# Operand offsets, kept output weights, a sixth early gate/up tile and the place of the second norm's sums in a fp32 decoder layer

## The chip, the cores and the metric

The kernel runs on one NeuronCore of a Trainium2 chip. The metric is the device time of one execution in microseconds, from the first instruction to the last and what the launch adds around them. The kernel before was timed in three runs.

## What is computed

One decoder layer over 512 positions with 2048 channels, in fp32. It takes a norm, projects to q, k, v and u, mixes with attention (8 heads) and with a state space model that a gate follows, projects both halves back with `w_out`, and adds to the residual `h`. Then follow the second norm, a gated MLP of 5632 channels, and the final norm:

```python
hn = _rmsnorm(h, norm1_g)
q, k, v, u = jnp.split(hn @ w_in, [1024, 2048, 3072], axis=-1)
attn_out = _dilated_attention_mixer(q, k, v, cos, sin)
ssm_out = _s5_mixer(u, ...)          # y * sigmoid(y @ w_glu + b_glu)
h = h + jnp.concatenate([attn_out, ssm_out], axis=-1) @ w_out
hn = _rmsnorm(h, norm2_g)
h = h + (jax.nn.silu(hn @ w_gate) * (hn @ w_up)) @ w_down
return _rmsnorm(h, final_g)
```

## The kernel before

**Layout and precision.** Activations lie transposed: 128 channels on the partitions, 512 positions in the free dimension. Every fp32 operand of a projection is held as two fp32r parts, hi and lo; `split` (lines 89 to 91) makes them, hi by a copy on ScalarE, lo by a subtraction on VectorE through the helper `tt` (line 50). `mm3` (lines 108 to 111) is then three matmuls: weights' hi against the activations' hi, hi against lo, lo against hi. So every weight costs a DMA, a copy on ScalarE and a subtraction on VectorE before TensorE has it.

**Slots.** Activations' hi and lo lie in slots of 1088 floats, given out by `laid` (pool, tag, count, offset) and `slot`; the last argument is the offset in floats at which the operand starts inside its slot. Offsets 0 and 48 are multiples of 16 floats (64 bytes); 4, 8, 40 and 52 are not. The text calls the first kind aligned and the second odd.

**Stages on TensorE**, in the order of time of the profiled execution: u, q, k and v to about 451 us, attention to 492 (pieces of it), `glu` 492 to 537 (operand `ysp`, offset 4), `oa` 537 to 627 (the attention half of `w_out`, operand `attn`, offset 8), `os0` and `os1` 627 to 723 (its other half, operand `ssm`, offset 40, for the first and the second 256 positions), then the MLP. `os0` and `os1` each load and split all 16 tiles of this half of `w_out`: `wchunk` (lines 103 to 106) loads 512 KB and splits it in two pieces of 512 columns.

**The second norm.** After each `os` tile the residual tile `h` gets the product on VectorE, ScalarE squares it, and GpSimd (`pool`) adds the square to the sums `ss2`. When a half is complete, `rstd_of` sums over the partitions with tiny matmuls (`ss_20`, `ss_21`, line 146), works out the reciprocal root on VectorE and ScalarE (`rst`), puts it on a diagonal (`dg`), and one matmul by a matrix of ones spreads it over the partitions (`bc`, line 159); ScalarE copies that to `rstd2`.

**The MLP.** Gate and up of a tile are made together by a scheme with seven products A to G of half the size, over operands `c1` (A, B), `c4` (C), `c2`, `c3` (D to G). Each product takes 24 matmuls of 256 columns, in two halves `hh` of 12. `c1` needs only the first half of the positions, so it is made in `first_half` during `os1`; `c2`, `c3` and `c4` need the second half. While these wait for the second norm, TensorE runs products A and B of the first NEARLY = 5 tiles (`gu_first`); weights of the first two are split ahead during `os1` (`split_early`). In the loop over `k` (the lines that follow `first = ...`), VectorE makes the normed pieces `x2` and `t34` (line 59), GpSimd makes four differences per k from them, and `split` makes `c2`, `c3`, `c4`. Then come the tiles' other products, and after every fourth tile the products with `w_down` (`dn`), 11 phases in all.

**What sets the order.** Engines run in order. The order on each is set by the tile scheduler from the program, by data dependences and the count of buffers in each tag; nothing in the kernel before fixes the place of the norm's matmuls among the products of `gu_first`.

## Time and profile before

| | |
|---|---|
| median of three runs | 2098.67 us (2095.85 to 2101.73) |
| the profiled execution's own time | 2100.22 us |
| its span, first to last instruction | 2098.4 us |
| mean granted TensorE clock | 0.986 |
| TensorE busy, matmuls | 2053.3 us (98%), 13522 instructions |
| VectorE busy | 1533.5 us (73%) |
| ScalarE busy | 865.5 us (41%) |
| GpSimd busy | 74.6 us (4%), 82 instructions |

The shares are means over the whole program. TensorE is busy nearly throughout; the rows to look for are those stretches where it is not, and those where its matmuls follow one another more slowly than elsewhere. In the traces a matmul's own duration covers its way through the array, so its rate is read from the distance of one start to the next. The same holds on VectorE, where one operation's end overlaps the next one's start.

### The profile page before, as it was taken

Reading aid. Unit: us, or ns where it says so; the run is one execution under the profiler, and the core shown is the slowest. Engines: PE = TensorE matmul, PEld = TensorE weight load, DVE = VectorE, ACT = ScalarE, POOL = GpSimd, SP = SyncE. Lnnn points to the kernel's source line nnn. Section 1 sums busy time; section 2 is a strip of 40 time slices with the busy share of each in tenths; the row PEclk is TensorE's granted clock in tenths of the full one; section 3 lists DMA queues with packets and bytes.
Section 4 is the critical chain, followed back from the end, with each engine's and each line's share of the span. In section 5 each row is a group of like instructions: output and inputs, shape, how many; then the busy total and the mean of one; then the engine's idle time right before and its main releaser. Section 6 shows DMA issues by size and latency. Waiting matters only on the chain.

```text
span 2098.4 us, 35067 instructions
## 1 busy us (share of the span) xinstructions
PE 2053.3 (98%) x13522; PEld 1859.9 (89%) x13522; DVE 1533.5 (73%) x2974; ACT 865.5 (41%) x1523; POOL 74.6 (4%) x82
## 2 busy tenths in 40 slices
PE   8999999999999979999999999999999999999996
PEld 6888888877889979899999989899998989999896
DVE  8845897565436899686786868687785868778686
ACT  6222222265225545353443525344353535444354
POOL 0000000000002360000000000000000000000002
PEclk9989999999999989999999999999999999999998
DMA  7533234424325523333232333323232332323232
GB/s 235 167 107 113 91 105 145 124 95 154 111 97 188 183 71 132 111 108 124 91 122 81 119 101 103 121 85 128 91 121 81 119 103 102 121 89 124 91 122 81
DMA packets 117192, 244.23 MB, mean 116 GB/s; under 512 B 39040, under 2 KB 57312, under 8 KB 117024
## 3 DMA queue, kind: packets, MB, share of 16 engines
q1 hardware_dynamic: 107808, 239.88, 34.0%
q10 hardware_dynamic: 9216, 2.10, 0.5%
q8 instruction: 106, 1.74, 0.3%
q14 instruction: 62, 0.51, 0.1%
HBM read 229.77 MB, written 9.03 MB: 114 GB/s over the span
## 4 chain that ended last, share of the span: by engine, by line
PE 91%; DVE 5%; issue 2%; ACT 1%; DMA 1%; POOL 0%; SPq 0%; DVEq 0%; ACTq 0%; POOLq 0%
PE gu L109 13%; PE gu L111 13%; PE gu L110 12%; PE dn L110 7%; PE dn L109 7%; PE dn L111 7%; PE q L111 1%; PE q L110 1%; PE u L109 1%; PE u L110 1%; PE lps L435 1%; PE q L109 1%; PE u L111 1%; PE oa L109 1%; PE oa L111 1%
## 5 line engine op out<-in xcount | busy, mean ns | idle before, releaser
L110 PE MATMUL dn<-m,whi_dn 128*128 128x512 f32 x640 | 249.0, 389 | 0.0
L111 PE MATMUL dn<-m,wlo_dn 128*128 128x512 f32 x640 | 248.8, 389 | 0.0
L109 PE MATMUL dn<-m,whi_dn 128*128 128x512 f32 x640 | 248.8, 389 | 0.0
L50 DVE TENSOR_TENSOR h<-h,dn 128x512 f32<-128x512 f32 x160 | 110.0, 687 | 172.5 <-PE dn L111 171.5
L90 ACT ACTIVATE whi_dn<-raw_dn 128x512 fp32r<-128x512 f32 x160 | 100.9, 632 | 240.1 <-PE dn L110 208.2
L50 DVE TENSOR_TENSOR raw_r<-raw_r,raw_r 128x512 f32<-128x512 f32 x264 | 182.8, 692 | 2.1
L111 PEld LDWEIGHTS dn<-m,wlo_dn 128*128 128x128 f32 x640 | 120.1, 188 | 25.0
L109 PEld LDWEIGHTS dn<-m,whi_dn 128*128 128x128 f32 x640 | 120.1, 188 | 24.6
L110 PEld LDWEIGHTS dn<-m,whi_dn 128*128 128x128 f32 x640 | 120.1, 188 | 24.5
L50 DVE TENSOR_TENSOR wlo_dn<-raw_dn,whi_dn 128x512 fp32r<-128x512 f32 x160 | 109.8, 687 | 17.2 <-ACT whi_dn L90 16.2
L109 PE MATMUL gu<-c,whi_D 128*128 128x256 f32 x352 | 98.4, 280 | 3.2 <-ACT whi_D L90 3.2
L109 PE MATMUL gu<-c,whi_C 128*128 128x256 f32 x352 | 99.8, 284 | 1.6 <-ACT c L90 1.6
L109 PE MATMUL gu<-c,whi_E 128*128 128x256 f32 x352 | 98.9, 281 | 2.5 <-ACT whi_F L90 1.1
L111 PE MATMUL gu<-c,wlo_E 128*128 128x256 f32 x352 | 98.8, 281 | 2.5 <-DVE wlo_E L50 2.4
L111 PE MATMUL gu<-c,wlo_D 128*128 128x256 f32 x352 | 98.7, 280 | 1.7 <-DVE wlo_D L50 1.7
L111 PE MATMUL gu<-c,wlo_C 128*128 128x256 f32 x352 | 99.5, 283 | 0.5 <-DVE wlo_C L50 0.5
L110 PE MATMUL gu<-c,whi_C 128*128 128x256 f32 x352 | 99.5, 283 | 0.1
L110 PE MATMUL gu<-c,whi_E 128*128 128x256 f32 x352 | 98.3, 279 | 0.0
L110 PE MATMUL gu<-c,whi_D 128*128 128x256 f32 x352 | 98.2, 279 | 0.0
L109 PE MATMUL gu<-c,whi_F 128*128 128x256 f32 x352 | 97.9, 278 | 0.0
L110 PE MATMUL gu<-c,whi_F 128*128 128x256 f32 x352 | 97.9, 278 | 0.0
L111 PE MATMUL gu<-c,wlo_F 128*128 128x256 f32 x352 | 97.7, 278 | 0.0
(317 smaller groups left out, 6462.1 us busy)
## 6 DMA issues: line engine op xcount, KB each, us to landing
raw_r<-w_gu SPq DMA_DIRECT2D x176, 512.0 KB, 3.5
raw_dn<-w_down SPq DMA_DIRECT2D x80, 512.0 KB, 4.0
raw_os<-w_out SPq DMA_DIRECT2D x32, 512.0 KB, 3.4
raw_q<-w_q SPq DMA_DIRECT2D x16, 512.0 KB, 4.1
raw_k<-w_k SPq DMA_DIRECT2D x16, 512.0 KB, 3.4
raw_v<-w_v SPq DMA_DIRECT2D x16, 512.0 KB, 3.8
raw_oa<-w_out SPq DMA_DIRECT2D x16, 512.0 KB, 3.5
raw_u<-w_u SPq DMA_DIRECT2D x15, 512.0 KB, 5.8
```

The source lines that it names most:

```text
L50: (eng or dve).tensor_tensor(out=out, in0=in0, in1=in1, op=op)
L90: act.activation(hi, raw, AF.Copy)
L109: pe.matmul(ps, wh, x[:, 0, :], start=first, stop=False)
L110: pe.matmul(ps, wh, x[:, 1, :], start=False, stop=False)
L111: pe.matmul(ps, wl, x[:, 0, :], start=False, stop=last)
L435: pe.matmul(lps[:, g, :], tm_[:, :, :, g].rearrange("p i q -> p (i q)"), U[:, 8 * b + g, :], start=True, stop=True)
```

## The change

1. **Offsets.** `ysp` goes from 4 to 0, `attn` from 8 to 0, `ssm` from 40 to 52 for the first two of eight and 48 for the others. `c4` went to offset 52 in all four slots; now only `c4_0` does, the single odd slot.
2. **Kept output weights.** Tiles 10 to 15 of the `ssm` half of `w_out` are split once, in `os0`, in pieces of 1024 columns, and kept; `os1` runs these six first and then tiles 0 to 9. Six loads of 512 KB and twelve pairs of 512-column splits go from `os1`.
3. **Sixth early tile.** NEARLY is 6. Tile 5 has no bank to keep, so ScalarE copies its A and B sums to `ev5`. Its 48 matmuls move ahead of the first tile's C. Three tiles' weights, not two, are split ahead during `os1`.
4. **The sums' place.** `rstd_of` marks the last sums matmul and the spread matmul. Products of half (0, 1) of the early tiles are issued after the sums, all later ones after the spread; those of (0, 0) are free.
5. **GpSimd's work.** The 30 additions to `ss2` and the 32 differences in the loop over `k` go to VectorE.

```diff
--- before.py
+++ after.py
@@ -1,6 +1,7 @@
 
 
 
+import contextlib
 import math
 
 import numpy as np
@@ -138,12 +139,14 @@
             act.activation(sq, src, AF.Square)
             tt(acc_t, acc_t, sq, ALU.add)
 
+    marks = {}
+
     def rstd_of(acc_t, out, name):
 
         n = acc_t.shape[-1] // 128
         ps = aux([128, 4], "ss_" + name)
         for m in range(n):
-            pe.matmul(ps[:, m:m + 1], acc_t[:, 128 * m:128 * m + 128], ones[:, 0:1], start=True, stop=True)
+            sums = pe.matmul(ps[:, m:m + 1], acc_t[:, 128 * m:128 * m + 128], ones[:, 0:1], start=True, stop=True)
         st = cpool.tile([128, 4, 4], F32, tag="rst", name="rst_" + name)
         v, q, r, c = (st[:, i, :n] for i in range(4))
         ts(v, ps[:, :n], 1.0 / D, EPS, ALU.mult, ALU.add)
@@ -156,7 +159,8 @@
         for m in range(n):
             ts(dg[:, m, :], ident, c[:, m:m + 1])
         bc = aux([128, 512], "bc_" + name)
-        pe.matmul(bc[:, :128 * n], ones, dg[:, :n].rearrange("p m t -> p (m t)"), start=True, stop=True)
+        spread = pe.matmul(bc[:, :128 * n], ones, dg[:, :n].rearrange("p m t -> p (m t)"), start=True, stop=True)
+        marks[name] = sums.ins, spread.ins
         act.activation(out, bc[:, :128 * n], AF.Copy)
         return c
 
@@ -560,7 +564,7 @@
     for b in range(8):
         yt = wpool.tile([128, 512], F32, tag="sq", name=f"yt{b}", bufs=4)
         nc.sync.dma_start(yt, sy[b].rearrange("p i c -> p (i c)"))
-        t_ = laid(ring2, "B", f"ysp{b}", 8, 4)
+        t_ = laid(ring2, "B", f"ysp{b}", 8, 0)
         split(t_[:, 0, :], t_[:, 1, :], yt)
         ysp.append(t_)
 
@@ -600,7 +604,7 @@
                 act.activation(PT[:, :w], tp[:, :w], AF.Copy)
             else:
                 pe.matmul(po[:, 128 * j:512], vs[j][:, 128 * h:128 * h + 128], PT[:, :w], start=j == 0, stop=j == 3)
-        o = slot("A0", f"attn{h}", 8)
+        o = slot("A0", f"attn{h}")
         act.activation(o[:, 0, :], po, AF.Copy)
         tt(o[:, 1, :], po, o[:, 0, :].bitcast(F32), ALU.subtract)
         attn.append(o)
@@ -616,7 +620,7 @@
         nc.sync.dma_start(yt, sy[f].rearrange("p i c -> p (i c)"))
         z = wpool.tile([128, NC_, T], F32, tag="sq", name=f"gz{f}", bufs=4)
         tt(z.rearrange("p c i -> p i c"), yt.rearrange("p (i c) -> p i c", i=T), g_.rearrange("p (i c) -> p i c", i=T), ALU.mult)
-        o = slot("A1", f"ssm{f}", 40)
+        o = slot("A1", f"ssm{f}", 52 if f < 2 else 48)
         split(o[:, 0, :], o[:, 1, :], z.rearrange("p c i -> p (c i)"))
         ssm.append(o)
     closed("v")
@@ -638,9 +642,20 @@
     rstd2 = ss2
     mp = opened("mlp", bufs=1)
 
+    KEEP = (10, 11, 12, 13, 14, 15)
+    kept = {}
+
+    def keep(f):
+        at = ("B", ring2, 8) if KEEP.index(f) < 4 else ("C", mp, 4)
+        hl = [laid(at[1], at[0], f"{t}_kept{f}", at[2], 0).rearrange("p a b -> p (a b)") for t in ("hi", "lo")]
+        raw = wraw(a["w_out"][2 * f + 1], f"os_{f}")
+        split(hl[0], hl[1], raw)
+        kept[f] = [[t[:, 512 * i:512 * i + 512] for t in hl] for i in range(2)]
+        return kept[f]
+
     def comb(tag, name, pool_=None, bufs=8):
 
-        return laid(pool_ or ring, tag, name, bufs, 52 if tag == "C" else 48).rearrange("p a (h t) -> p a h t", h=2)
+        return laid(pool_ or ring, tag, name, bufs, 52 if name == "c4_0" else 48).rearrange("p a (h t) -> p a h t", h=2)
 
     early = {}
 
@@ -654,7 +669,7 @@
         raw = load_first(f, hh)
         early[f, hh] = []
         for i in range(2):
-            t_ = laid(ring2, "B", f"w{'AB'[i]}{f}_{hh}", 8, 0)
+            t_ = laid(*((ring2, "B") if f < 2 else (mp, "C")), f"w{'AB'[i]}{f}_{hh}", 8 if f < 2 else 4, 0)
             split(t_[:, 0], t_[:, 1], raw[:, 512 * i:512 * i + 512])
             early[f, hh].append((t_[:, 0], t_[:, 1]))
 
@@ -674,28 +689,28 @@
         split(t_[:, :, 0, :], t_[:, :, 1, :], n1[k][0])
         c1.append(t_)
 
-    PRE = (2, 3, 4, 5)
-    AT = (4, 5, 6, 7, 8, 9, 10, 11)
+    PRE = (1, 2, 3, 4, 11, 12)
+    AT = (3, 4, 5, 6, 7, 8, 9, 10)
     for e in range(2):
         es = E[e]
-        for f in range(KT):
+        for i, f in enumerate(KEEP + tuple(range(KEEP[0])) if e else range(KT)):
             ps = acc(f"os{e}_{f}")
-            ws = wchunk(a["w_out"][2 * f + 1], f"os{e}_{f}")
+            ws = (kept[f] if e else keep(f)) if f in KEEP else wchunk(a["w_out"][2 * f + 1], f"os{e}_{f}")
             for k in range(8):
                 hi, lo = ws[k // 4]
                 sl = slice(128 * (k % 4), 128 * (k % 4) + 128)
                 mm3(ps[:, 0:256], hi[:, sl], lo[:, sl], ssm[k][:, :, es], k == 0, k == 7)
             tt(h[f][:, es], h[f][:, es], ps[:, 0:256], ALU.add)
-            if f == 0:
+            if i == 0:
                 act.activation(ss2[:, es], h[f][:, es], AF.Square)
             else:
                 sq = wpool.tile([128, 512], F32, tag="sq", name=f"sq_h{e}_{f}", bufs=4)[:, 0:256]
                 act.activation(sq, h[f][:, es], AF.Square)
-                tt(ss2[:, es], ss2[:, es], sq, ALU.add, pool)
-            if e == 1 and f in PRE:
-                split_early(PRE.index(f) // 2, PRE.index(f) % 2)
-            if e == 1 and f in AT:
-                first_half(AT.index(f))
+                tt(ss2[:, es], ss2[:, es], sq, ALU.add)
+            if e == 1 and i in PRE:
+                split_early(PRE.index(i) // 2, PRE.index(i) % 2)
+            if e == 1 and i in AT:
+                first_half(AT.index(i))
         rstd_of(ss2[:, es], rstd2[:, es], f"2{e}")
 
     PR = {1: (c1, 0), 2: (c1, 1), 3: (c2, 0), 7: (c2, 1), 5: (c3, 0), 6: (c3, 1), 4: (c4, None)}
@@ -720,15 +735,21 @@
     def gu_first(f):
 
         bk = bank(f"gu{f}_0")
+        sums, spread = marks["21"]
         for hh in range(2):
             if (f, hh) in early:
                 wa, wb = early[f, hh]
             else:
                 raw = load_first(f, hh)
                 wa, wb = wsplit(raw[:, W0], f"A{f}_{hh}"), wsplit(raw[:, W1], f"B{f}_{hh}")
-            product([bk], 1, hh, *wa)
-            product([bk], 2, hh, *wb)
-        return bk
+            with tc.issue_after(sums if (f, hh) == (0, 1) else spread) if (f, hh) != (0, 0) else contextlib.nullcontext():
+                product([bk], 1, hh, *wa)
+                product([bk], 2, hh, *wb)
+        if f < NBANK:
+            return bk
+        out = wpool.tile([128, 512], F32, tag="ev", name=f"ev{f}")
+        act.activation(out, bk, AF.Copy)
+        return out
 
     def gu(f, bank0=None):
         banks = [bank0 or bank(f"gu{f}_0")] + [bank(f"gu{f}_{i}") for i in range(1, 4)]
@@ -766,7 +787,8 @@
         split(o[:, 0, :], o[:, 1, :], g_)
         return o
 
-    NEARLY = 5
+    NEARLY = 6
+    NBANK = 5
     NPH = 11
     first = [gu_first(f) for f in range(NEARLY)]
     for k in range(8):
@@ -774,14 +796,14 @@
         x_, y_, z_ = (wpool.tile([128, 2, 256], F32, tag="sq", name=f"{n}_{k}", bufs=4) for n in ("x2", "t12", "t34"))
         norm(x_[:, 0], k + 8, es)
         norm(z_[:, 0], k, es)
-        tt(x_[:, 1], x_[:, 0], z_[:, 0], ALU.subtract, pool)
+        tt(x_[:, 1], x_[:, 0], z_[:, 0], ALU.subtract)
         t2 = comb("B", f"c2_{k}", ring2)
         split(t2[:, :, 0, :], t2[:, :, 1, :], x_)
-        tt(y_[:, 0], z_[:, 0], n1[k][0][:, 0], ALU.subtract, pool)
-        tt(y_[:, 1], x_[:, 0], y_[:, 0], ALU.subtract, pool)
+        tt(y_[:, 0], z_[:, 0], n1[k][0][:, 0], ALU.subtract)
+        tt(y_[:, 1], x_[:, 0], y_[:, 0], ALU.subtract)
         t3 = comb("A1", f"c3_{k}")
         split(t3[:, :, 0, :], t3[:, :, 1, :], y_)
-        tt(z_[:, 1], n1[k][0][:, 1], y_[:, 1], ALU.subtract, pool)
+        tt(z_[:, 1], n1[k][0][:, 1], y_[:, 1], ALU.subtract)
         if k % 2 == 0:
             t4 = comb("C", f"c4_{k}", mp, 4)
             c4.append(t4)
```

How this moves instructions, at three places. On TensorE before, at the sums of the second half (`gu0` is the first early tile, `c1` its operand):

```order
L109 MATMUL gu0_0_6935<-c1_7_6760,wA0_1_6383 128x256
L110 MATMUL gu0_0_6935<-c1_7_6760,wA0_1_6383 128x256
L111 MATMUL gu0_0_6935<-c1_7_6760,wA0_1_6383 128x256
L146 MATMUL ss_21_6919<-ones_71,ss2_5575 128x1 x2
L109 MATMUL gu0_0_6935<-c1_4_6627,wB0_1_6386 128x256
L110 MATMUL gu0_0_6935<-c1_4_6627,wB0_1_6386 128x256
```

The sums stand behind the 36 matmuls of products A and B of the first tile's first half and A of its second; the spread matmul `bc_21` stands 37 matmuls further on. On TensorE after:

```order
L111 MATMUL os1_9_6814<-ssm7_4981,whi_os1_9_1_6821 128x256
L112 MATMUL os1_9_6814<-ssm7_4981,wlo_os1_9_1_6822 128x256
L112 MATMUL gu0_0_6869<-c1_2_6415,wB0_0_6255 128x256
L110 MATMUL gu0_0_6869<-c1_3_6459,wB0_0_6255 128x256
L111 MATMUL gu0_0_6869<-c1_3_6459,wB0_0_6255 128x256
L112 MATMUL gu0_0_6869<-c1_3_6459,wB0_0_6255 128x256
L149 MATMUL ss_21_6853<-ones_71,ss2_5575 128x1 x2
L110 MATMUL gu0_0_6869<-c1_4_6504,wA0_1_6290 128x256
L111 MATMUL gu0_0_6869<-c1_4_6504,wA0_1_6290 128x256
```

Of the 24 matmuls of tile 0's first half, 20 now stand inside `os1`, and four between its last matmul and the sums; the spread matmul stands 24 matmuls further on, and the other five early tiles' 240 matmuls behind it. On VectorE before, from the diagonal of the second norm on (`x2` and `t34` are the normed pieces, `wlo_` the low parts of weights):

```order
L54 TENSOR_SCALAR dg_21_6929<-ident_70,rst_21_6922 128x128 x2
L50 TENSOR_TENSOR wlo_B3_0_7113<-raw_g3_0_7105,whi_B3_0_7112 128x512
L50 TENSOR_TENSOR wlo_A3_1_7144<-raw_g3_1_7140,whi_A3_1_7143 128x512
L59 SCALAR_TENSOR_TENSOR x2_0_7246<-h_4990,g2_67,ss2_5575 128x256
L59 SCALAR_TENSOR_TENSOR t34_0_7248<-h_4990,g2_67,ss2_5575 128x256
L59 SCALAR_TENSOR_TENSOR x2_1_7264<-h_4990,g2_67,ss2_5575 128x256
L50 TENSOR_TENSOR c2_0_7252<-x2_0_7246,c2_0_7252 128x2x256
L59 SCALAR_TENSOR_TENSOR t34_1_7266<-h_4990,g2_67,ss2_5575 128x256
L50 TENSOR_TENSOR c3_0_7257<-t12_0_7247,c3_0_7257 128x2x256
```

The four differences per k are not in this list, as they run on GpSimd. On VectorE after, up to the first step of the reciprocal root:

```order
L51 TENSOR_TENSOR ss2_5575<-ss2_5575,sq_h1_7_6772 128x256
L51 TENSOR_TENSOR h_4990<-h_4990,os1_9_6814 128x256
L51 TENSOR_TENSOR wlo_A4_0_7092<-raw_g4_0_7088,whi_A4_0_7091 128x512
L51 TENSOR_TENSOR ss2_5575<-ss2_5575,sq_h1_8_6811 128x256
L51 TENSOR_TENSOR ss2_5575<-ss2_5575,sq_h1_9_6850 128x256
L57 TENSOR_SCALAR rst_21_6856<-ss_21_6853 128x2
```

The last two additions of squares now stand behind a split of `gu4` weights on VectorE. And from the diagonal on:

```order
L55 TENSOR_SCALAR dg_21_6863<-ident_70,rst_21_6856 128x128 x2
L60 SCALAR_TENSOR_TENSOR x2_0_7231<-h_4990,g2_67,ss2_5575 128x256
L60 SCALAR_TENSOR_TENSOR t34_0_7233<-h_4990,g2_67,ss2_5575 128x256
L51 TENSOR_TENSOR x2_0_7231<-x2_0_7231,t34_0_7233 128x256
L51 TENSOR_TENSOR t12_0_7232<-t34_0_7233,n1_0_6334 128x256
L60 SCALAR_TENSOR_TENSOR x2_1_7249<-h_4990,g2_67,ss2_5575 128x256
L51 TENSOR_TENSOR t12_0_7232<-x2_0_7231,t12_0_7232 128x256
L51 TENSOR_TENSOR c2_0_7237<-x2_0_7231,c2_0_7237 128x2x256
L51 TENSOR_TENSOR t34_0_7233<-n1_0_6334,t12_0_7232 128x256
```

No weights' split stands between the diagonal and `x2_0` any more, and the subtractions that GpSimd had stand between the normed pieces and the splits.

## Rows read from the trace of the kernel before

**Rows 1.** The page, part 1: busy time, share of the span and instructions.

```profile
PE 2053.3 (98%) x13522; PEld 1859.9 (89%) x13522; DVE 1533.5 (73%) x2974; ACT 865.5 (41%) x1523; POOL 74.6 (4%) x82
```

**Rows 2.** Stretches: us, busy time (instructions) PE PEld DVE ACT POOL, granted clock, DMA share, GB/s.

```profile
676.00:733.20 57.20, 55.24 (x456) 54.10 (x455) 48.89 (x94) 34.10 (x68) 16.84 (x16) 1.00 0.54 186
733.20:784.00 50.80, 39.81 (x262) 37.00 (x261) 47.03 (x65) 22.84 (x42) 33.62 (x32) 0.81 0.20 66
784.00:844.00 60.00, 57.81 (x478) 56.37 (x478) 57.59 (x107) 30.59 (x51) 0.00 (x0) 0.99 0.38 137
```

**Rows 3.** Timeline about the second norm, all engines: start, us, engine, line, operation.

```profile
722.92 0.28 PE L109 MATMUL gu<-c,wA 128*128 128x256 f32 x1
...
724.93 0.41 DVE L50 TENSOR_TENSOR h<-h,os 128x256 f32<-128x256 f32 x1
...
726.00 0.73 POOL L50 TENSOR_TENSOR ss<-ss,sq_h 128x256 f32<-128x256 f32 x1 [1.53 <-ACT sq_h L693]
...
727.16 0.50 PE L146 MATMUL ss<-ones,ss 128*128 128x1 f32 x4
...
728.99 0.48 DVE L54 TENSOR_SCALAR dg<-ident,rst 128x128 f32<-128x128 f32 x2
...
731.97 0.60 PE L159 MATMUL bc<-dg,ones 128*128 128x256 f32 x2
...
733.25 0.48 DVE L59 SCALAR_TENSOR_TENSOR x<-h,g,ss 128x256 f32<-128x256 f32 x1
```

**Rows 4.** VectorE's groups by form from 733.2 to 784: busy, mean ns | idle before.

```profile
L50 DVE TENSOR_TENSOR c<-x,c 128x512 fp32r<-128x512 f32 x8 | 7.7, 957 | 3.0 <-ACT c L90 3.0
...
L50 DVE TENSOR_TENSOR c<-t,c 128x256 fp32r<-128x256 f32 x8 | 5.5, 683 | 0.0
```

**Rows 5.** Timeline of VectorE from 766 to 771.

```profile
769.37 0.68 DVE L50 TENSOR_TENSOR wlo_C<-raw_r,whi_C 128x512 fp32r<-128x512 f32 x1
769.97 0.41 DVE L50 TENSOR_TENSOR c<-t,c 128x256 fp32r<-128x256 f32 x1
770.31 0.68 DVE L50 TENSOR_TENSOR raw_r<-raw_r,raw_r 128x512 f32<-128x512 f32 x1
```

**Rows 6.** Timeline of VectorE at the end of the stretch.

```profile
844.18 0.69 DVE L50 TENSOR_TENSOR wlo_G<-raw_r,whi_G 128x512 fp32r<-128x512 f32 x1 [0.18 <-ACT whi_G L90]
```

**Rows 7.** Tiles k, oa, glu and os on TensorE: ns min/median/max, first and last start.

```profile
L110 PE MATMUL k<-x,whi_k x113: 389/389/389, 261.7 to 337.9; 128*128 128x512 f32 x113
...
L109 PE MATMUL oa<-attn,whi_oa x128: 391/395/397, 537.6 to 626.5; 128*128 128x512 f32 x128
...
L110 PE MATMUL glu<-ysp,whi_glu x50: 390/394/398, 499.7 to 533.7; 128*128 128x512 f32 x50
...
L109 PE MATMUL os<-ssm,whi_os x130: 282/283/283, 629.4 to 675.8; 128*128 128x256 f32 x130
```

**Rows 8.** Timeline of TensorE in a later tile: first matmul of A, C, B and D.

```profile
909.65 0.28 PE L109 MATMUL gu<-c,whi_A 128*128 128x256 f32 x1
...
911.01 0.28 PE L109 MATMUL gu<-c,whi_C 128*128 128x256 f32 x1
...
912.43 0.28 PE L109 MATMUL gu<-c,whi_B 128*128 128x256 f32 x1
...
913.81 0.28 PE L109 MATMUL gu<-c,whi_D 128*128 128x256 f32 x1
```

**Rows 9.** Timeline of TensorE after a wait, from 806 to 810.

```profile
806.37 0.36 PE L109 MATMUL gu<-c,whi_E 128*128 128x256 f32 x1 [0.75 <-ACT whi_G L90]
806.57 0.28 PE L110 MATMUL gu<-c,whi_E 128*128 128x256 f32 x1
...
808.34 0.28 PE L109 MATMUL gu<-c,whi_C 128*128 128x256 f32 x1
...
809.39 0.28 PE L109 MATMUL gu<-c,whi_F 128*128 128x256 f32 x1
...
809.61 0.28 PE L111 MATMUL gu<-c,wlo_F 128*128 128x256 f32 x1
```


## The prediction

> **What bounds the kernel now.** I read the page's part 1 first: TensorE is busy for 2053.3 of 2098.4 us [rows 1], so a change can win in two ways only: by filling TensorE's remaining holes, or by making the matmuls follow one another faster. Where the holes are is read from the busy time by stretches [rows 2]. From 676 to 733.2 (`os1` and the first early products) TensorE lacks 57.20 - 55.24 = 2.0 us. From 733.2 to 784 it lacks 11.0 us, its granted clock is 0.81 on average, and it gets through 262 matmuls where the next 60 us hold 478. VectorE is busy there for 47.03 of 50.80 us, and from 784 to 844 for 57.59 of 60.00. So from the second norm to the first `dn` VectorE sets the time. The timeline about the norm [rows 3] shows how this stretch begins: `os1`'s last matmul gives way to the next product at 722.92, the residual's last addition starts at 724.93, GpSimd's last square is added at 726.00, the sums go through TensorE at 727.16, the diagonal is started at 728.99, the spread matmul at 731.97, and `x2_0`, the first piece that all the rest hangs on, at 733.25. VectorE's last split before `dn` starts at 844.18 [rows 6]. For the rate I read starts of matmuls [rows 7 to 9].
>
> For scale: a difference of 0.3% or 6.3 us is about what a measurement of this kernel can tell from no change.
>
> **VectorE from `x2_0` to that last split, 110.9 us (844.18 - 733.25).** Its busy time there is 47.03 + 57.59 = 104.6 us, so 6.3 us are idle. Part of the busy time is not work: while GpSimd runs its 32 differences (33.62 us busy, [rows 2]) VectorE's operations are longer. The subtraction for `c2` takes 957 ns in the mean, the one for `c4` 683 [rows 4]; alone, shapes of 512 columns take 0.68 and of 256 columns 0.41 us [rows 5]. These two groups exceed that by 8 x 0.28 + 8 x 0.27 = 4.4 us, and by the same subtraction the other nine groups of this view that are longer than their form alone by 9.2, in all 13.6 us. Without GpSimd's operations this goes, and 91.0 us of work stay. Added are 32 differences of 256 columns at 0.34 each, the distance of starts from 769.97 to 770.31 [rows 5], 10.9 us; four splits for the sixth early tile at 0.60 (769.37 to 769.97), 2.4 us. Two splits leave for `os1`, -1.2 us. That makes 103.1 us. Of the 6.3 us of idle time 3.0 are waits of the `c2` subtraction for a ScalarE copy, which stands behind GpSimd's difference [rows 4]; that wait goes, but the differences hang on one another, so I keep 4.3 us. The new length is 107.4 us: **-3.5 us**. The bounds: no idle time left gives -7.8, all of it kept -1.5.
>
> Here a rule can be weighed. The rows show operations of 512 columns going from 0.68 to 0.96 us in the mean beside GpSimd, some 13.6 us against 33.62 us of GpSimd's work. The Trainium skill, "SBUF — State Buffer", section "SBUF: two separate sides", says that VectorE with two SBUF inputs and GpSimd hold a shared pair of ports exclusively, and that the other fully blocks for the whole instruction. By that alone up to 33.6 us would come back in place of 13.6, and the total below would be 20.0 us lower, an estimate by that page of 2058. The trace agrees that one delays the other, but VectorE was held up for less than half of GpSimd's busy time, so the sum goes by the rows.
>
> **From `os1`'s end to `x2_0`, 10.3 us before (722.92 to 733.25).** After, the order has on VectorE the residual's addition, one split and two additions of squares ahead of the sums: about 0.4 us for the last matmul to end, then 0.34 + 0.60 + 2 x 0.34, so the sums start near 2.2 us, and not at 4.2 (727.16). Only four matmuls cover this on TensorE, so it waits some 1.7 us; the path runs over VectorE, and this wait is inside the 2.2. From the sums to the diagonal's start it was 1.83 us (727.16 to 728.99) plus 0.48 for the diagonal itself; the spread matmul stood behind 37 products and began at 4.8 us after the sums. Those were (4.8 - 0.4) / 37 = 0.119 us apart; now it stands behind 24, 2.8 us, with 0.4 for the sums: 3.2 us. From there to `x2_0` it is 1.28 us as before. Sum: 2.2 + 3.2 + 1.3 = 6.7 us, **-3.6 us**. Bounds: the spread at once when the diagonal is ready, -4.5; the two additions late by one more split and their ScalarE squares, -1.
>
> **The products that move.** The sixth tile's 48 matmuls go from the bound-by-TensorE stretch behind the first `dn` into the one that VectorE bounds, where TensorE had 11.0 us of holes: 48 x 0.113 = -5.4 us. Its four splits are in the sum above. The 20 matmuls of tile 0 that now stand inside `os1` delay its end by 20 x 0.113 = +2.3 us, since they are no longer cover for the norm. Together **-3.1 us**. ScalarE's copy to `ev5` (about a 0.6 us operation) and its later use cost nothing on the path: ScalarE is busy for 30.59 of 60 us there; without that cover it would be 0.6.
>
> **`os1` and `os0`.** Twelve splits of 512 columns leave `os1` on VectorE (12 x 0.60 = 7.2 us), 15 additions of squares come (15 x 0.34 = 5.1), and GpSimd no longer stretches anything. In `os0` six splits of 1024 columns take the place of twelve, and 15 additions come, 5.1 us over 49 us in which VectorE has room. Six loads of 512 KB less on SP's queue are hidden either way, the DMA share being 0.54. Of the 2.0 us of TensorE's holes [rows 2] I take half: **-1.0 us** (bounds -2.0 and +1).
>
> **Offsets.** In the k stage, whose operand is aligned, one of three matmuls starts from 261.7 to 337.9 us over 112 steps: 76.2 / 336 = 226.8 ns a matmul. In `oa`, at offset 8, 88.9 / 381 = 233.3; in `glu`, at offset 4, 34.0 / 147 = 231.3 [rows 7]. At the aligned rate `oa`'s 384 matmuls gain 2.5 us and `glu`'s 192 gain 0.9. The same for 256 columns: `os0` 46.4 / 387 = 119.9 ns [rows 7], against (911.01 - 909.65) / 12 = 113.3 for an aligned product A [rows 8]. `os0`'s six aligned slots of eight would gain 288 x 6.6 ns = 1.9 us; `os1` ran faster already and keeps its odd slots' share, so I take 1.8 for both (bounds 0 and 3). In a steady tile C takes 1.42 and B behind it 1.38 in place of 1.36 us per half [rows 8], 0.16 us a tile; with one odd slot of four only one half keeps about 0.05. For the 39 tiles whose four slots all count, that is 39 x 0.11 = 4.3 us. Together **-9.5 us** (bounds 0 and -12.6).
>
> **The sum** against the profiled execution's own 2100.22 us: -3.5 - 3.6 - 3.1 - 1.0 - 9.5 = -20.7, so 2079.5. That execution is 1.55 us above the median of the runs shown, so on the median's footing the forecast is **2078.0 us**.
>
> **The rivals.**
>
> *Only the rate pays.* The norm's chain and VectorE's stretch end no earlier, because ScalarE or the chain of dependent differences takes GpSimd's place. For it: 3.0 us of VectorE's waits were already for ScalarE [rows 4]. Against it: ScalarE is busy for under half of either stretch [rows 2]. It gives 2098.7 - 9.5 = 2089.2.
>
> *Offsets are without effect* and the slower rates have another cause, such as what else the core reads. For it: the aligned products between the sums and the spread start 0.119 us apart too [rows 3]. Against it: C and B differ from A inside one tile [rows 8]. The rest gives -11.2, so 2087.5.
>
> *VectorE is simply full.* The longer operations come from something other than GpSimd, and the 32 differences are added without return: 104.6 + 6.3 + 12.1 = 123.0 us, so +12.1 in place of -3.5, and the sum is -5.1 or 2093.6, no change that can be told. Against it: from 784 on, with GpSimd idle, the operations are short. The Trainium skill, "Perfetto Trace Analysis", section "Optimizing Scalar/DVE Operations", advises to take work off a saturated VectorE, to ScalarE or even GpSimd, though it adds that between VectorE and GpSimd a move might not help because of the shared port. The trace so far bears out the second half.
>
> *Slower: one odd slot does not bring the fast rate back.* After a wait of 0.75 us TensorE ran aligned matmuls of E and F at (808.34 - 806.57) / 15 = 0.118 us; behind two C matmuls with odd slots at 808.34 the rate came back, and stands at 0.11 from 809.39 on [rows 9]. If one odd slot in a tile's first half is too little, the 39 tiles' 168 matmuls run at 118 in place of 113.3 ns: 39 x 168 x 4.6 ns = 30.1 us, less the 6.2 that the odd slots cost today, +23.9. With -11.2 and -3.4 for `oa` and `glu` that is +9.3: 2108.0. It decides from the point where six odd matmuls a tile, those of C's first half on `c4_0`, no longer end what a wait began. Against it: after E two odd matmuls and less than a microsecond were enough.
>
> **Chances.** Forecast 0.64; only the rate 0.12; offsets without effect 0.08; still faster, below the range 0.03; VectorE full 0.08; slower by the lost rate 0.05. The first four make faster 0.87; same 0.08; slower 0.05. Low end: all lower bounds at once (VectorE -4.3, norm -0.9, `os` -1.0, offsets -3.1 below their terms) give 2068.7; TensorE's granted clock, 0.81 in the stretch, may recover with fewer holes, for which I go on to 2066. High end: the slower of the two faster rivals, 2089.2, with the 2.0 us by which VectorE's term can be worse: 2091. What lies outside is 0.03 + 0.08 + 0.05 = 0.16.
>
> **What would show it.** In the profile after: `x2_0` some 6.7 us behind `os1`'s end; VectorE's operations of 512 columns at 0.68 from the norm on; the last split of the stretch 107 us later; `oa` at 227 ns a matmul, C and B at 1.36 us a half; GpSimd idle in the stretch; `gu5`'s A and B ahead of `gu0`'s C. Wrong would be: steady products at 118 ns, VectorE's idle time over 8 us in the stretch, or the sums later than 3 us behind `os1`'s end. A granted clock at the lower of its two levels, 1.2 GHz, over more of the stretch than the 0.81 of before implies would show that the holes were closed too little to keep it up.

## The result and the profile after

The changed kernel takes 2074.16 us (2072.84 to 2076.46, four runs) against 2098.18 us of the kernel before (four runs): a ratio of 0.9884, 95% interval 0.9872 to 0.9896, or 24.0 us less. Forecast were 2078.0 us and -20.7 us. The spans of the two profiled executions differ by 25.5 us, and the stretches from one start to the next in the two traces say where:

| from start to start | before | after | difference | forecast |
|---|---|---|---|---|
| first instruction to first `glu` | 492.21 | 491.53 | -0.68 | 0 |
| first `glu` to first `oa` | 45.44 | 44.54 | -0.89 | -0.9 |
| first `oa` to first `os` | 89.60 | 87.04 | -2.56 | -2.5 |
| first to last `os` | 95.56 | 92.25 | -3.31 | -1.8 - 1.0 + 2.3 = -0.5 |
| last `os` to `x2_0` | 10.45 | 8.47 | -1.98 | -3.6 |
| `x2_0` to the last split before `dn` | 110.93 | 103.87 | -7.06 | -3.5 |
| that split to the first `dn` | 1.51 | 1.60 | +0.09 | 0 |
| first `dn` to the second phase's first | 121.59 | 115.68 | -5.91 | together |
| second phase's first to the tenth's | 963.52 | 960.10 | -3.42 | -5.4 - 4.3 = -9.7 |
| tenth phase's first to the end | 167.63 | 167.81 | +0.18 | 0 |

Part 1 of the page after, to be held against [rows 1]:

```profile
PE 2035.2 (98%) x13522; PEld 1846.9 (89%) x13522; DVE 1524.3 (74%) x3018; ACT 857.8 (41%) x1506; POOL 11.3 (1%) x20
```

TensorE is 18.1 us less busy with the same 13522 matmuls, so part of the gain is matmuls that follow one another faster. GpSimd has 20 instructions left of 82.

The stretches after, from `os1` to the last split before `dn` (us, then busy time and instructions of TensorE, its weight loads, VectorE, ScalarE and GpSimd, granted clock, DMA share, GB/s), answer to [rows 2]:

```profile
668.00:715.50 47.50, 47.50 (x410) 47.45 (x410) 43.98 (x96) 31.94 (x63) 0.00 (x0) 1.00 0.55 185
715.50:723.80 8.30, 6.50 (x41) 6.14 (x40) 3.52 (x13) 1.64 (x4) 0.00 (x0) 0.79 0.24 85
723.80:774.60 50.80, 47.31 (x375) 45.62 (x374) 50.66 (x110) 27.89 (x49) 0.00 (x0) 0.93 0.25 84
774.60:827.70 53.10, 51.76 (x441) 50.64 (x441) 52.04 (x97) 27.77 (x49) 0.00 (x0) 1.00 0.40 140
```

In `os1` TensorE has no hole any more. Behind the norm it gets through 375 matmuls in 50.8 us, where it was 262. VectorE is busy for 50.66 of 50.80 and 52.04 of 53.10 us: the stretch is bound by VectorE as before, but VectorE idles for 1.2 us in it and not for 6.3. In the 8.3 us around the norm the granted clock is 0.79; in [rows 2] the stretch with `os1`'s end and the norm stood at 1.00. In the 50.8 us behind it the clock is 0.93, where it was 0.81.

The timeline about the norm after (start, duration, engine, line, operation, idle time before and its releaser), to be held against [rows 3]:

```profile
715.36 0.28 PE L112 MATMUL os<-ssm,wlo_os 128*128 128x256 f32 x1
...
715.87 0.41 DVE L51 TENSOR_TENSOR h<-h,os 128x256 f32<-128x256 f32 x1
...
716.28 0.69 DVE L51 TENSOR_TENSOR wlo_A<-raw_g,whi_A 128x512 fp32r<-128x512 f32 x1
...
716.88 0.95 DVE L51 TENSOR_TENSOR ss<-ss,sq_h 128x256 f32<-128x256 f32 x2
...
717.89 0.61 PE L149 MATMUL ss<-ones,ss 128*128 128x1 f32 x4 [1.79 <-DVE ss L51]
...
719.75 0.49 DVE L55 TENSOR_SCALAR dg<-ident,rst 128x128 f32<-128x128 f32 x2
...
720.25 0.41 PE L112 MATMUL gu<-c,wB 128*128 128x256 f32 x1
...
720.46 0.41 PE L110 MATMUL gu<-c,wB 128*128 128x256 f32 x1
...
722.38 0.99 PE L162 MATMUL bc<-dg,ones 128*128 128x256 f32 x2
...
723.83 0.48 DVE L60 SCALAR_TENSOR_TENSOR x<-h,g,ss 128x256 f32<-128x256 f32 x1 [3.60 <-ACT ss L164]
```

The sums wait 1.79 us for VectorE's additions of squares, and while the diagonal is being made the granted clock falls: the products between the sums and the spread matmul start 0.21 us apart (720.25, 720.46) in place of 0.114. That is the lower of the clock's two levels, 1.2 in place of 2.4 GHz. So the spread matmul starts 4.49 us behind the sums, though only 24 products stand between; it was 4.81 with 37 [rows 3].

VectorE's groups by form from 723.8 to 774.6 (busy, mean ns | idle before), answering to [rows 4], and the last split before `dn`, answering to [rows 6]:

```profile
L51 DVE TENSOR_TENSOR c<-x,c 128x512 fp32r<-128x512 f32 x8 | 5.5, 686 | 0.0
...
L51 DVE TENSOR_TENSOR c<-t,c 128x256 fp32r<-128x256 f32 x8 | 3.3, 421 | 0.0
```

```profile
827.70 0.69 DVE L51 TENSOR_TENSOR wlo_G<-raw_r,whi_G 128x512 fp32r<-128x512 f32 x1 [0.18 <-ACT whi_G L91]
```

The subtraction for `c2` is at 686 ns in place of 957 and the one for `c4` at 421 in place of 683. The differences that GpSimd had stand among VectorE's operations from `x2_0` on (`t` is `t34` or `t12`):

```profile
724.24 0.48 DVE L60 SCALAR_TENSOR_TENSOR t<-h,g,ss 128x256 f32<-128x256 f32 x1
724.75 0.43 DVE L51 TENSOR_TENSOR x<-x,t 128x256 f32<-128x256 f32 x1
725.09 0.42 DVE L51 TENSOR_TENSOR t<-t,n 128x256 f32<-128x256 f32 x1
725.42 0.48 DVE L60 SCALAR_TENSOR_TENSOR x<-h,g,ss 128x256 f32<-128x256 f32 x1
725.82 0.42 DVE L51 TENSOR_TENSOR t<-x,t 128x256 f32<-128x256 f32 x1
```

A difference takes 0.34 us from start to start (724.75 to 725.09). Where one needs the operation just before it, it starts 0.11 us late: 0.51 us behind `t34` (724.24 to 724.75), where 0.40 us separate operations that do not hang on each other (725.42 to 725.82).

The rate of `oa` and of `glu`, as in [rows 7], and the first matmuls of A, C, B and D of a tile that follows `dn`, as in [rows 8]:

```profile
L110 PE MATMUL oa<-attn,whi_oa x128: 389/389/389, 536.1 to 622.4; 128*128 128x512 f32 x128
...
L112 PE MATMUL glu<-ysp,wlo_glu x51: 389/389/389, 499.8 to 533.8; 128*128 128x512 f32 x51
```

```profile
1108.53 0.28 PE L110 MATMUL gu<-c,whi_A 128*128 128x256 f32 x1
...
1109.94 0.28 PE L110 MATMUL gu<-c,whi_C 128*128 128x256 f32 x1
...
1111.37 0.28 PE L110 MATMUL gu<-c,whi_B 128*128 128x256 f32 x1
...
1112.73 0.28 PE L110 MATMUL gu<-c,whi_D 128*128 128x256 f32 x1
```

Both 512-column stages are at (622.4 - 536.1) / 381 = 226.5 and (533.8 - 499.8) / 150 = 226.7 ns a matmul. The tile shows something finer: A takes 1.41 us, C with its odd slot 1.43, and from B on twelve matmuls take 1.36. So the first product behind `dn` runs at 0.118 us a matmul, and 0.113 comes back with the odd slot in C.

### The profile page after: what moved, and what is told of

Read it like the earlier page. It is cut to its first block, busy times and chain, and to the rows that moved or that the text cites. A ratio compares the mean times of both kernels' runs of the same rounds, so it can differ in the third digit from the quotient of the medians.

```text
span 2072.9 us, 34928 instructions
## 1 busy us (share of the span) xinstructions
PE 2035.2 (98%) x13522; PEld 1846.9 (89%) x13522; DVE 1524.3 (74%) x3018; ACT 857.8 (41%) x1506; POOL 11.3 (1%) x20
## 4 chain that ended last, share of the span: by engine, by line
PE 92%; DVE 4%; DMA 2%; ACT 2%; issue 1%; SPq 0%; DVEq 0%; ACTq 0%
PE gu L110 13%; PE gu L111 12%; PE gu L112 12%; PE dn L111 7%; PE dn L110 7%; PE dn L112 7%; PE q L112 2%; PE q L111 1%; PE lps L439 1%; PE q L110 1%; PE v L556 1%; PE os L110 1%; PE v L557 1%; PE v L558 1%; PE os L111 1%; PE k L110 1%
```

## The experiments

The theory is that of the forecast's sum: each part pays in its own stage. The rivals are those of the prediction, above all "VectorE is simply full", "offsets are without effect" and "one odd slot does not bring the fast rate back". The changed kernel was not timed again beside these runs, so its time beside each is taken as 0.9884 of the kernel before there: 2075.6 us for the first four (before: 2099.95), 2074.4 for the next four (2098.73), 2075.7 for the last four (2100.09), each uncertain by 2.5 us. Where that is too coarse, the stretches of the table above decide, of which `glu`, `oa` and the phases repeat to 0.05 us between profiles with the same offsets; the first row varies by 4 us and the last by 2.

**Old offsets in the changed kernel.**

```diff
-        t_ = laid(ring2, "B", f"ysp{b}", 8, 0)
+        t_ = laid(ring2, "B", f"ysp{b}", 8, 4)
-        o = slot("A0", f"attn{h}")
+        o = slot("A0", f"attn{h}", 8)
-        o = slot("A1", f"ssm{f}", 52 if f < 2 else 48)
+        o = slot("A1", f"ssm{f}", 40)
-        return laid(pool_ or ring, tag, name, bufs, 52 if name == "c4_0" else 48).rearrange("p a (h t) -> p a h t", h=2)
+        return laid(pool_ or ring, tag, name, bufs, 52 if tag == "C" else 48).rearrange("p a (h t) -> p a h t", h=2)
```

> The changed kernel with the four offsets of before (ysp 4, attn 8, ssm 40, all c4 at 52), the rest as changed. Theory of the sum (every part pays in its own stage): glu +0.9, oa +2.6, os +2.2, C and B of the steady tiles +3.4 to 4.2, together +9 to +10 on 2074.2, so 2083 to 2084; oa back at 233 ns a matmul. Rival, offsets without effect: 2074 within 2 us and oa at 227. Rival, the odd slots cost more in the stretch behind the norm than in the steady tiles: over 2086.

2084.29 us, ratio to before 0.993 (0.9916 to 0.9945): 8.7 us over the changed kernel. The row of `oa` in its trace:

```profile
L110 PE MATMUL oa<-attn,whi_oa x128: 392/395/398, 535.0 to 623.9; 128*128 128x512 f32 x128
```

That is (623.9 - 535.0) / 381 = 233.3 ns, the rate of before. The stretches: `glu` +0.88, `oa` +2.56, `os` +2.51, the eight later phases +0.43 each. This is the theory's result, in every stage.

**New offsets alone in the kernel before.**

```diff
-        t_ = laid(ring2, "B", f"ysp{b}", 8, 4)
+        t_ = laid(ring2, "B", f"ysp{b}", 8, 0)
-        o = slot("A0", f"attn{h}", 8)
+        o = slot("A0", f"attn{h}")
-        o = slot("A1", f"ssm{f}", 40)
+        o = slot("A1", f"ssm{f}", 52 if f < 2 else 48)
-        return laid(pool_ or ring, tag, name, bufs, 52 if tag == "C" else 48).rearrange("p a (h t) -> p a h t", h=2)
+        return laid(pool_ or ring, tag, name, bufs, 52 if name == "c4_0" else 48).rearrange("p a (h t) -> p a h t", h=2)
```

> The kernel before with the four new offsets and nothing else. Theory of the sum: the same 9 to 10 us off 2098.2, so 2088 to 2089. If the offsets pay only because VectorE and the norm were made faster as well: under half of that, 2094 or more. Offsets without effect: 2098.

2090.75 us against 2099.95, ratio 0.9959 (0.9947 to 0.9972): -9.2 us. `os` shortens by 1.68 us here, `glu` and `oa` as in the changed kernel. The offsets' term stands by itself and needs none of the other parts.

**The differences back on GpSimd.**

```diff
-        tt(x_[:, 1], x_[:, 0], z_[:, 0], ALU.subtract)
+        tt(x_[:, 1], x_[:, 0], z_[:, 0], ALU.subtract, pool)
...
```

The same for the other three differences of each k.

> The changed kernel with the 32 differences back on GpSimd; the squares stay on VectorE. Theory (GpSimd stretches VectorE and its results come late): from x2_0 to the last split before dn 103.9 us lose 10.9 of differences, gain 13.6 of stretch and 3 to 5 of waits: +6 to +8, so 2080 to 2082, and operations of 512 columns on VectorE near 0.95 in the mean. Rival (VectorE is simply full, its long operations are not GpSimd's doing): -10.9, so 2063.

2083.56 us, ratio 0.9925 (0.991 to 0.994): 8.0 us over the changed kernel. From `x2_0` to the last split it is 112.34 us in place of 103.87. The first 51 us of that, and two of VectorE's groups in them:

```profile
721.00:772.00 51.00, 42.48 (x316) 40.57 (x316) 45.59 (x63) 22.85 (x42) 31.77 (x32) 0.90 0.19 63
```

```profile
L51 DVE TENSOR_TENSOR c<-x,c 128x512 fp32r<-128x512 f32 x8 | 7.2, 896 | 3.4 <-ACT c L91 3.4
...
L51 DVE TENSOR_TENSOR c<-t,c 128x256 fp32r<-128x256 f32 x8 | 5.5, 683 | 0.0
```

The long operations are back at 896 and 683 ns, and with them 3.4 us of waiting for ScalarE's copies, as in [rows 4]. VectorE loses 10.9 us of differences and the stretch still grows by 8.5, so 19.4 us come with GpSimd's 31.77 us of work. Of these 13.4 us are longer operations: VectorE is busy for 105.2 us in the stretch, where 102.7 less 10.9 is 91.8. The longer operations come to some four tenths of GpSimd's time. The rest is waiting, for ScalarE's copies and for GpSimd's results. The Trainium skill, "SBUF — State Buffer", section "SBUF: two separate sides", by whose rule the loser blocks for the whole instruction, would have had up to all of GpSimd's time come; the measurement agrees that one delays the other, but by less than that.

**The differences alone on VectorE, in the kernel before.**

```diff
-        tt(x_[:, 1], x_[:, 0], z_[:, 0], ALU.subtract, pool)
+        tt(x_[:, 1], x_[:, 0], z_[:, 0], ALU.subtract)
...
```

> The kernel before with the 32 differences on VectorE and nothing else. Theory: the stretch of 110.9 us becomes 91.0 + 10.9 and 1 to 4 us of idle time, 103 to 106, so -5 to -8: 2090 to 2093. Rival (VectorE is simply full): +10.9, so 2109. Rival (ScalarE or the chain of differences takes GpSimd's place): 2098 within 2 us.

2092.24 us, ratio 0.9966 (0.9955 to 0.9978): -7.7 us. The stretch is 103.66 us in place of 110.93. VectorE in it:

```profile
733.00:784.00 51.00, 42.54 (x295) 38.69 (x294) 50.76 (x110) 26.02 (x48) 0.00 (x0) 0.87 0.26 84
784.00:836.70 52.70, 52.36 (x445) 51.70 (x446) 51.03 (x95) 27.45 (x47) 0.00 (x0) 1.00 0.42 139
```

It is busy for 50.76 + 51.03 = 101.8 of 103.70 us. Before it was 104.6 without the 10.9 us of differences, so 13.7 us of longer operations went with GpSimd's work, and the prediction had 13.6. "VectorE is simply full" forecast +10.9 and falls: the long operations were GpSimd's doing, and this one edit alone brings more than the prediction gave the whole term. "Only the rate pays" falls with it.

**No odd slot.**

```diff
-        o = slot("A1", f"ssm{f}", 52 if f < 2 else 48)
+        o = slot("A1", f"ssm{f}", 48)
-        return laid(pool_ or ring, tag, name, bufs, 52 if name == "c4_0" else 48).rearrange("p a (h t) -> p a h t", h=2)
+        return laid(pool_ or ring, tag, name, bufs, 48).rearrange("p a (h t) -> p a h t", h=2)
```

> The changed kernel with no odd slot at all: c4_0 and all ssm at 48. Theory (after a wait the aligned matmuls stay slow until an odd operand comes by): the wait at the spread and those in the stretch leave everything at 0.118 us a matmul, in the steady tiles up to 39 x 168 x 4.6 ns = 30 us: over 2080 and up to 2106. Rival (an aligned operand is all that counts, the odd slot is a remnant): 2 us less for C's first half, 2072 to 2074.

2102.49 us, ratio to before 1.0015 (1.0006 to 1.0025): 28 us over the changed kernel and slower than the kernel before. First matmuls of A and, three products later, of D in a tile that follows `dn`:

```profile
1117.33 0.28 PE L110 MATMUL gu<-c,whi_A 128*128 128x256 f32 x1
...
1121.57 0.28 PE L110 MATMUL gu<-c,whi_D 128*128 128x256 f32 x1
```

Each product takes 1.41 us (4.24 for three), and every product of every later tile does: the matmuls of 256 columns start 0.118 us apart to the end of the phase. The phases take 122.67 us in place of 120.01. `oa`, with 512 columns, is at 87.04 us here too. So the slow rate is one that fully aligned matmuls of 256 columns can keep for a whole phase, and one odd slot ends it. This is the mechanism of the rival that I gave 0.05. Its price of 30.1 us, against tiles without a slow product, is near the 28 measured against the changed kernel; its point of decision was not reached, since the six odd matmuls of `c4_0` do suffice. Without the last odd slot the offsets turn a gain of 9 us into a loss of 19.

An odd operand is not the only thing that ends the slow rate. In this run, which has none, it ended at the hole ahead of the sums:

```profile
716.71 0.28 PE L111 MATMUL os<-ssm,whi_os 128*128 128x256 f32 x1
...
717.65 0.28 PE L112 MATMUL gu<-c,wB 128*128 128x256 f32 x1
719.71 0.60 PE L149 MATMUL ss<-ones,ss 128*128 128x1 f32 x4 [1.77 <-DVE ss L51]
...
726.39 0.28 PE L110 MATMUL gu<-c,wB 128*128 128x256 f32 x1
...
727.75 0.28 PE L110 MATMUL gu<-c,wA 128*128 128x256 f32 x1
```

Ahead of the hole matmuls start (717.65 - 716.71) / 8 = 0.118 us apart, behind it (727.75 - 726.39) / 12 = 0.113. A wait of 0.75 us did the opposite in [rows 9]. So the rate can change either way at a wait of TensorE, and the odd slot counts in the phases, which have no wait.

**Five early tiles.**

```diff
-    NEARLY = 6
+    NEARLY = 5
```

> The changed kernel with five early tiles. Theory of the sum: the 48 products return to the stage that TensorE bounds, +5.4, and four splits leave the stretch that VectorE bounds, -2.4: +3.0, so 2077 to 2078. Rival (TensorE bounds the stretch after the change too): 0, so 2074 to 2075. Rival (ScalarE's copy to ev5 costs): below 2074.

2078.85 us, ratio 0.9902 (0.9888 to 0.9917): 4.4 us over the changed kernel, where 3.0 were expected. From the first `dn` to the second phase it takes 121.17 us, +5.49, the 48 products that come back. The splits that leave shorten VectorE's stretch by 0.70 only, where 2.4 were expected: VectorE is busy for 1.7 us less there (100.97 us) and idles for 2.2 us in place of 1.2. Why it idles more is open. And the clock held at the norm here, though the hole at the sums is the same:

```profile
718.96 0.61 PE L149 MATMUL ss<-ones,ss 128*128 128x1 f32 x4 [1.79 <-DVE ss L51]
...
722.34 0.60 PE L162 MATMUL bc<-dg,ones 128*128 128x256 f32 x2
```

The spread matmul stands 3.38 us behind the sums, with the same 24 products that took until 4.49 in the changed kernel.

**Nothing kept.**

```diff
-        for i, f in enumerate(KEEP + tuple(range(KEEP[0])) if e else range(KT)):
+        for i, f in enumerate(range(KT)):
-            ws = (kept[f] if e else keep(f)) if f in KEEP else wchunk(a["w_out"][2 * f + 1], f"os{e}_{f}")
+            ws = wchunk(a["w_out"][2 * f + 1], f"os{e}_{f}")
```

> The changed kernel without kept output weights: os1 loads and splits all 16 tiles again, in order 0 to 15. Theory (the second os half was bound by VectorE): twelve splits of 0.60 come back on a VectorE that is 93% busy there (43.98 of 47.50 us): some 4 us of TensorE waits, 2077 to 2079. Rival (splits and loads there are hidden): 2074 to 2075, and no TensorE wait on wlo_os.

2079.93 us, ratio 0.9905 (0.989 to 0.9919): 5.5 us over. First to last `os` takes 95.97 us, +3.72. TensorE's waits from 670 to 720 (total us, times, longest):

```profile
PE bc L162 <- DVE dg L55: 1.2, 1, 1.2
PE os L112 <- DVE wlo_os L51: 0.8, 1, 0.8
PE os L110 <- ACT whi_os L91: 0.5, 2, 0.3
```

The waits for `dg`, `wlo_os` and `whi_os` of `os1` are back, none of which the changed kernel has. They show as 2.5 us. By distances of starts, what TensorE loses in `os1` beyond 0.12 us a matmul, it is more: 4.2 us, where the changed kernel loses 0.5, since matmuls right behind a wait also start late.

**The order left free.**

```diff
-            with tc.issue_after(sums if (f, hh) == (0, 1) else spread) if (f, hh) != (0, 0) else contextlib.nullcontext():
+            with contextlib.nullcontext():
```

> The changed kernel with the products' place left free; in its order the sums then stand 43 matmuls later and the spread 38 behind them, where it is 24. Theory (what stands ahead of the norm's matmuls delays all of VectorE's stretch): the sums begin some 5 us behind os1's end in place of 2.5, x2_0 3 to 4 us later, 2077 to 2079; against that the granted clock does not fall at the sums, which gives back 1.3. Rival (the norm's place is hidden by the early products): 2074 to 2075.

2080.05 us, ratio 0.9906 (0.9891 to 0.9921): 5.6 us over. `os1`'s last matmul starts at 716.68; then, on TensorE and VectorE:

```profile
722.12 0.50 PE L149 MATMUL ss<-ones,ss 128*128 128x1 f32 x4
...
727.98 0.49 DVE L60 SCALAR_TENSOR_TENSOR x<-h,g,ss 128x256 f32<-128x256 f32 x1 [3.62 <-ACT ss L164]
```

The sums stand 5.44 us behind `os1`'s end in place of 2.52 and `x2_0` 11.30 in place of 8.47. VectorE waits for the spread and nothing makes up for it. The clock stayed at its upper level.

**Three attempts to do better, and the squares.** The first puts all 24 products of tile 0's first half behind `os1`, as cover for the sums (`marks["os"]` is the last `os1` matmul):

```diff
-            with tc.issue_after(sums if (f, hh) == (0, 1) else spread) if (f, hh) != (0, 0) else contextlib.nullcontext():
+            with tc.issue_after(marks["os"] if (f, hh) == (0, 0) else sums if (f, hh) == (0, 1) else spread):
```

> The changed kernel with all 24 products of tile 0's first half issued after os1's last matmul, so that they stand between it and the sums. Theory (VectorE's chain sets the sums, the products inside os1 only delay it, and the hole of 1.8 us at the sums lets the granted clock fall): os1 ends 2.3 us earlier, the hole goes, the clock stays, x2_0 comes 1.4 to 3.7 us earlier: 2070.5 to 2073. Rival (VectorE has no room to take the end of os1 earlier): the wait at the sums stays and x2_0 with it, 2074 to 2075.

2077.94 us, ratio 0.989 (0.9877 to 0.9904): no better. `os1` ends 2.3 us earlier, but:

```profile
717.51 0.61 PE L149 MATMUL ss<-ones,ss 128*128 128x1 f32 x4 [1.81 <-DVE ss L51]
...
722.16 0.86 PE L162 MATMUL bc<-dg,ones 128*128 128x256 f32 x2
```

The sums wait 1.81 us as before, the clock falls again, and from the first `os` to `x2_0` it takes 100.77 us in place of 100.72. The rival was right: VectorE, busy for 43.98 of 47.50 us ahead of the norm, sets the time of the sums, and TensorE's order there is free within these 2.3 us.

The second leaves one odd matmul a tile, the low part of the second k of `c4_0`:

```diff
+        t = mp.tile([128, SLOT], F32R, tag="C", name=name, bufs=4)
+        return [t[:, 48:560].rearrange("p (h t) -> p h t", h=2), t[:, 560:1080].rearrange("p (h t) -> p h t", h=2)[:, :, 0:256]]
```

> The changed kernel with a single odd operand in the tiles: of c4_0 only the low part of the second k starts at an odd offset, one matmul a tile. Theory (the first odd matmul ends the slow rate, and each further one only costs): C's first half falls from 1.43 to 1.37 us, 44 tiles, -2 to -3: 2071 to 2072.5. Rival (several in a row are needed): steady tiles at 0.118, near 2102.

2078.78 us, ratio 0.9899 (0.9885 to 0.9912): 3.1 us worse, a miss for both sides. C, B and D of a tile behind `dn`, then of the next one (from 1128.75):

```profile
1108.96 0.28 PE L110 MATMUL gu<-c,whi_C 128*128 128x256 f32 x1
...
1110.38 0.28 PE L110 MATMUL gu<-c,whi_B 128*128 128x256 f32 x1
...
1111.79 0.28 PE L110 MATMUL gu<-c,whi_D 128*128 128x256 f32 x1
...
1128.75 0.28 PE L110 MATMUL gu<-c,whi_C 128*128 128x256 f32 x1
...
1130.14 0.28 PE L110 MATMUL gu<-c,whi_B 128*128 128x256 f32 x1
...
1131.50 0.28 PE L110 MATMUL gu<-c,whi_D 128*128 128x256 f32 x1
```

In the first tile the single odd matmul does not end the slow rate (B still takes 1.41 us), in the second it does (B 1.36), and so it is in every phase. From there C takes 1.36 to 1.37 us, as hoped. But a phase takes 120.55 us, 0.54 more. One odd matmul is not always enough; six were in every phase of the changed kernel. What the lost phases cost, 8 x 0.54 = 4.3 us, is more than the 1.6 us by which `x2_0` comes nearer to `os1`, as the clock held at the norm here.

The third had both edits:

> Both edits, the covered sums and the one odd matmul. If they are independent: the sum of the two gains, 2068 to 2071.

2082.64 us, ratio 0.9915 (0.9901 to 0.9928), 6.9 us worse. Its `os` takes 90.20 us as in the first attempt and its phases 120.55 as in the second; the two do not help together either. With the order of the first attempt the clock held here, and the spread matmul stood 3.29 us behind the sums in place of 4.66.

Last, the additions of squares back on GpSimd:

```diff
-                tt(ss2[:, es], ss2[:, es], sq, ALU.add)
+                tt(ss2[:, es], ss2[:, es], sq, ALU.add, pool)
```

> The changed kernel with the 30 additions of squares back on GpSimd. Theory (GpSimd's operations stretch VectorE wherever it is full): 15 of them in os1, 5.1 us less on VectorE against some 6 us of stretch, and the last one comes later: os1 and the way to x2_0 0 to 3 us longer, 2074 to 2077. Rival (VectorE relieved is what counts): below 2073.

2076.35 us, ratio 0.9884 (0.987 to 0.9897), that of the change itself. TensorE's waits from 620 to 720:

```profile
PE os L110 <- ACT whi_os L91: 1.4, 2, 1.2
PE os L112 <- DVE wlo_os L51: 0.5, 1, 0.5
PE ss L149 <- POOL ss L51: 0.2, 1, 0.2
```

`os` grows by 1.42 us, with waits for splits, although 12 of the 20 products of tile 0 left `os1` in this run's order and now stand in front of the sums. `x2_0` comes 1.81 us nearer to `os1`'s end, as the hole at the sums shrinks to 0.2 us and the clock holds. The stretch behind is 2.1 us longer. In all, the move of the squares is not seen in the time; as the order moved with it, this run does not show the squares by themselves.

## Why the prediction was right, point by point

The signs were right in every stage of the table, and two runs show the two largest mechanisms by themselves: -9.2 us for the offsets alone and -7.7 us for the differences alone. Three terms were mis-sized. Two of the errors add up and the third works against them, so that the sum is closer than its terms: 3.3 us, with single terms up to 3.6 off.

**VectorE from `x2_0` on, -3.5 forecast, -7.1 measured.** The step that failed is "the differences hang on one another, so I keep 4.3 us" of idle time. They do hang on one another, but that costs 0.11 us where one needs the operation just before it, other work stands between most of them, and 1.2 us of idle time were left. The work was right: 103.1 us forecast, 50.66 + 52.04 = 102.7 measured. My lower bound, no idle time at all, was -7.8.

**From `os1`'s end to `x2_0`, -3.6 forecast, -2.0 measured.** The steps up to the sums held: 2.5 us behind the end where 2.2 were forecast, with TensorE waiting 1.79 where 1.7 were. What failed is "this wait is inside the 2.2". In the profiled execution the granted clock fell behind it, and the 24 products behind the sums took until 4.49 us, where 3.2 were worked out at the upper level. In the three runs with this order in which the clock held it was 3.28 (old offsets, one odd matmul) and 3.38 (five early tiles), and `x2_0` came 6.85 to 6.95 us behind `os1`: the 6.7 of the forecast.

**`os0` and `os1`, -2.8 forecast without the 20 products, -5.6 measured.** The offsets' 1.8 lies between -1.68 alone and the +2.51 of the run that undoes them. What failed is "of the 2.0 us of TensorE's holes I take half". All of them went, and they were worth more than the busy time by stretches shows: by distances of starts TensorE lost 3.8 us in `os1` before and 0.5 after. Without kept weights 3.7 us come back. The other 2.3 of the 5.6 us are the rate.

**The products that move and the later tiles' offsets, -9.7 forecast, -9.1 measured** in the three last rows. The five-tile run gives 5.49 for the 48 products, and the phases give 0.427 for four tiles, 0.107 a tile where 0.11 was forecast.

Undone one by one the parts cost 8.7, 8.0, 4.4, 5.5 and 5.6 us, 32 in all, against 24. Much of this excess can be the changed kernel's reference time, whose 2.5 us stand in each of the five; by the stretches, without the first and the last row, it is 28 against 25. What excess is left has two reasons that can be named, but no run separates them: the run with the free order is not the order of before, as 20 products of tile 0 stay inside `os1` and the sums come behind 47 matmuls there; and kept weights make the room on VectorE that the squares need.

Of the rivals, "VectorE is simply full" and "offsets are without effect" fell to measurements of their own. "Only the rate pays" fell with the differences alone. Of "one odd slot does not bring the fast rate back" the slow rate is real, and without the last odd slot it cost 28 us; but one slot did bring the fast rate back.

## What to carry to other kernels

Read a matmul's rate from the distance of starts, stage by stage and operand by operand, and compare like shapes: 4 to 6 ns in 113 or 227 were worth 9 us here, at no cost in work. Work on an idle engine is not free if that engine and the busy one hold each other up: 10.9 us of additions on a full VectorE saved 7.7 us. When the order ahead of a chain is tightened, look at what the new hole does to the granted clock, and on which engine the chain really waits, before moving cover there.

## What the runs showed of the hardware that was not expected

- Matmuls of 256 columns with fully aligned operands have two rates that last: 0.113 and 0.118 us from start to start. Behind the 512-column matmuls of `dn` they began at 0.118 in every phase, and with no odd operand they stayed there to the next `dn`; with the odd slot they went to 0.113 behind it. A wait of TensorE started the slow rate in [rows 9] and ended it in the run without an odd slot. An odd matmul itself takes about 0.119. Matmuls of 512 columns showed one rate when aligned, 226.7 ns, and 231 to 233 when not. Why an odd operand ends the slow rate, and which waits do, is open; no run here shows it.
- A single odd matmul ended the slow rate in the second tile of every phase, and not in the first; six close together did so in the first tile of every phase.
- After the same hole of 1.8 us on TensorE, with the same order around it, the granted clock fell to the lower level in four profiles (the changed kernel, differences on GpSimd, no odd slot, nothing kept) and stayed up in three (old offsets, five early tiles, one odd matmul). In the five profiles without such a hole (the kernel before, offsets alone, differences alone, free order, squares on GpSimd) it stayed up there. So the hole seems to be needed for the fall, but what decides it is open. In the start of the spread matmul it is worth 1.1 to 1.6 us each time, so such a difference in a single execution is no proof of an edit.
